# A hybrid convolution and gating layer: seven block products for eight, short filters for the convolution, and the out-projection in two passes

## The chip, the cores and the metric

The kernel runs on one core of a Trainium2 chip. A core has a matrix engine (TensorE, PE in the profile, with PEld for its weight loads), a vector engine (VectorE, DVE), a scalar engine (ScalarE, ACT), GpSimd (POOL) and SyncE (SP), which here only issues DMA transfers. Each engine runs its own list of instructions in order and waits on semaphores for the others. The metric is the device time of one execution in microseconds (us), lower is better; a comparison of two versions of this kernel counts as a difference from 0.2% on.

## The reference

One layer over 2048 tokens of width 1024, in fp32:

```
h = rms_norm(x, norm_g) * (1 + scale) + shift          # scale, shift, gate = silu(c) @ w_ada + b_ada
a, a_glu, a_gate, u, v, b_gate = split(h @ w_in)       # six column blocks of 1024 each
a   = a * sigmoid(a_glu)
a   = depthwise_conv(a, conv_w, 31 taps, centred) + conv_b
y_a = silu(layer_norm(a, ln_g, ln_b)) * silu(a_gate)
v   = layer_norm(v, sg_ln_g, sg_ln_b)                  # over the 1024 channels
v   = w_s[head] @ v + b_s                              # in chunks of 128 tokens, 8 heads of 128 channels
y_b = u * v * silu(b_gate)
x   = x + gate * (concat(y_a, y_b) @ w_out)            # w_out: 2048 x 1024
out = rms_norm(x, final_g)
```

## The kernel before

Every fp32 operand of a large product is split in two float32r parts, `hi` (an ACT copy) and `lo` (the rest, a DVE subtraction); a product is three matmuls, hi*hi, hi*lo and lo*hi, accumulated in one PSUM bank. One matmul takes 128 channels of weights and up to 512 tokens (or 128 tokens and 512 output columns).

The tokens are worked in two halves of 1024. `hhi` and `hlo` hold h of one half, channels on partitions. For every half:

- `v_group` (L254, matmuls at L243 to L245): v with tokens on partitions, in two column halves of eight banks each, 192 matmuls each.
- `conv_in(hf, j)` (L277) for each of 8 channel chunks j: `load_split` brings the weights of a_glu and a (two 512 KB loads, ACT copy at L120, DVE subtraction at L121), `proj` (L232 to L234) makes the columns. The first half takes 1040 tokens in blocks of 352, 352 and 336, since the filter reaches 15 tokens beyond, the second half 1008 in two blocks of 504.
- `conv(hf, j, g)` (L300): one ACT instruction for the first tap and 30 DVE instructions over 1024 tokens (L304) for the others.
- `gmlp(hf, j)`: b_gate (`pb`) and u (`pu`) in two blocks of 512, eight small fp32 matmuls `px` (L363) with w_s.
- `tail_of_half`: `conv_gate` (a_gate, `pag`), `conv_norm`, then the out-projection in groups of 2, 3 and 3 token tiles (L386 to L388). Each group loads and splits all of w_out again (16 chunks of 512 KB), the last group of the second half excepted.

All results between the stages stay on chip (`CY`, `VY`, `SQ`). The order on each engine is made when the program is built, by a list scheduler with costs of its own and priorities from the code; the start of the first half is ordered by hand on DVE.

Of the kernel before, what the change touches and what calls it, by code (L numbers as in the profile page):

```python
# [11 lines left out]
ALU = mybir.AluOpType  # L12

P = 128
D = 1024
KC = D // P
S = 2048
T = 1024
NTT = T // P
HALO = 16  # L20
TH = T + HALO
# [4 lines left out]
OFF = 1000  # L26
G0S, G0N, G1S = 0, 1, 4
# [3 lines left out]
def hybrid_layer_kernel(  # L31
# [20 lines left out]
    nc = tc.nc  # L52

    const = ctx.enter_context(tc.tile_pool(name="const", bufs=1))
    wst = ctx.enter_context(tc.tile_pool(name="wst", bufs=3))
    wsp = ctx.enter_context(tc.tile_pool(name="wsp", bufs=2))
    gpool = ctx.enter_context(tc.tile_pool(name="gpool", bufs=3))
    epool = ctx.enter_context(tc.tile_pool(name="epool", bufs=3))
    tabs = ctx.enter_context(tc.tile_pool(name="tabs", bufs=1))
    work = ctx.enter_context(tc.tile_pool(name="work", bufs=2))  # L60
    small = ctx.enter_context(tc.tile_pool(name="small", bufs=4))
    psum = ctx.enter_context(tc.tile_pool(name="psum", bufs=6, space=bass.MemoryType.PSUM))
    psumx = ctx.enter_context(tc.tile_pool(name="psumx", bufs=2, space=bass.MemoryType.PSUM))
# [7 lines left out]
    def wk(name, dt=F32):  # L71
        return work.tile([P, NG], dt, tag="wk", name=name)

    def ek(name, dt=F32):
        return epool.tile([P, 1056], dt, tag="e", name=name)

    def gk(name):
        return gpool.tile([P, 1056], F32, tag="g", name=name)

    tab = {}  # L80

    def load_wsT(hf):
        t = tabs.tile([P, KC, P], F32, tag="tab", name=f"wsT_{hf}")
        nc.sync.dma_start(t, w_sT)
        tab["wsT"] = t

    def load_fg(hf):
        t = tabs.tile([P, D], F32, tag="tab", name=f"fg_{hf}")
        nc.sync.dma_start(t, final_g.partition_broadcast(P))
        tab["fg"] = t  # L90
# [9 lines left out]
    btab = const.tile([P, KC, P], F32, name="btab")  # L100
    gate_b = const.tile([P, D], F32, name="gate_b")
# [5 lines left out]
    sv = const.tile([P, KC, 2 * PAD + 1], F32, name="sv")  # L107
    vst = const.tile([P, 4, NTT], F32, name="vst")

    hhi = const.tile([P, KC, TH], F32R, name="hhi")  # L110
    hlo = const.tile([P, KC, TH], F32R, name="hlo")
    CY = const.tile([P, KC, T], F32, name="CY")
    VY = const.tile([P, KC, T], F32, name="VY")
    SQ = const.tile([P, T], F32, name="SQ")

    normg, convb, clg, clb, slg, slb = (cols_sb[:, i, :] for i in range(6))

    def split(hi, lo, src, offset=OFF):
        with tc.high_priority(offset=offset):
            nc.scalar.activation(hi, src, AF.Copy)  # L120
            return nc.vector.tensor_tensor(out=lo, in0=src, in1=hi.bitcast(F32), op=ALU.subtract).ins  # L121

    def load(src, name):
        st = wst.tile([P, 1024], F32, tag="wst", name=f"st_{name}")
        nc.sync.dma_start(st, src)
        return st

    def split_w(st, a, name, offset=OFF):
        hi = wsp.tile([P, 1024], F32R, tag="whi", name=f"hi_{name}")
        lo = wsp.tile([P, 1024], F32R, tag="wlo", name=f"lo_{name}")  # L130
        split(hi, lo, st, offset)
        return hi.rearrange("p (a b) -> p a b", a=a), lo.rearrange("p (a b) -> p a b", a=a)

    def load_split(src, a, name):
        return split_w(load(src, name), a, name)

    nothing = lambda sqrt: None

    def rstd_of(var, n, name, np=P, fill=nothing):
        tile = lambda what: sm(f"{what}_{name}", n)[:np]  # L140
        sd, r0, t0, t1, r1 = (tile(what) for what in ("sd", "r0", "t0", "t1", "r1"))
        sqrt = nc.scalar.activation(sd, var, AF.Sqrt).ins
        fill(sqrt)
        nc.vector.reciprocal(out=r0, in_=sd)
        nc.vector.tensor_tensor(out=t0, in0=r0, in1=r0, op=ALU.mult)
        nc.vector.scalar_tensor_tensor(out=t1, in0=t0, scalar=-0.5, in1=var, op0=ALU.mult, op1=ALU.mult)
        nc.vector.scalar_tensor_tensor(out=r1, in0=t1, scalar=1.5, in1=r0, op0=ALU.add, op1=ALU.mult)
        return r1

    def spread(r, n, dst, name):  # L150
        """dst: the columns of r, one per 128 tokens, as rows on every partition."""
        ns = n // P
        dg = wk(f"dg_{name}")
        nc.vector.tensor_tensor(
            out=dg.rearrange("p (s t) -> p s t", t=P)[:, :ns, :],
            in0=ident[:, None, :].broadcast_to([P, ns, P]),
            in1=r[:, :, None].broadcast_to([P, ns, P]),
            op=ALU.mult,
        )
# [3 lines left out]
        return pr[:, :n]  # L163

    def rstd_rows(ssum, n, dst, name):
        """dst: 1/sqrt(mean + eps) of the columns of ssum summed over partitions, on every partition."""
        ns = n // P
        with tc.high_priority(offset=OFF):
            pc = xbank(f"pc_{name}")
            for s in range(ns):  # L170
                nc.tensor.matmul(pc[:, s : s + 1], ssum[:, s * P : s * P + P], ones[:, 0:1], start=True, stop=True)
            var = sm(f"var_{name}", ns)
            nc.vector.tensor_scalar(out=var, in0=pc[:, :ns], scalar1=1.0 / D, scalar2=EPS, op0=ALU.mult, op1=ALU.add)
            spread(rstd_of(var, ns, name), n, dst, name)

# [1 line left out]
    def mod_load(k):  # L177
        for i in range(2):
            nc.sync.dma_start(VY[:, (2 * k + i) % KC, :], wa_ss[i * KC + k])

    pms = {}

    def mod_half(k, i):
        if i == 0:
            pms[k] = sm(f"pm_{k}", 2)
        w = VY[:, (2 * k + i) % KC, :]
        nc.vector.scalar_tensor_tensor(
            out=w, in0=w, scalar=1.0, in1=c_row, op0=ALU.mult, op1=ALU.mult, accum_out=pms[k][:, i : i + 1]
        )
        if i == 1:  # L190
            nc.vector.tensor_tensor(out=mod[:, k, :], in0=pms[k], in1=bss_sb[:, k, :], op=ALU.add)
            nc.vector.scalar_tensor_tensor(
                out=gsc[:, k : k + 1],
                in0=mod[:, k, 1:2],
                scalar=1.0,
                in1=normg[:, k : k + 1],
                op0=ALU.add,
                op1=ALU.mult,
            )
# [526 lines left out]
    for hf in range(2):  # L726
# [15 lines left out]
        if hf == 0:  # L742
            x1_rstd()
# [69 lines left out]
```

## Time and profile before

| | |
|---|---|
| median of 3 runs | 1520.37 us (1520.12 to 1520.76) |
| profiled execution, first to last instruction | 1518.9 us |
| PE busy | 1490.1 us, 98% |
| DVE busy | 1189.2 us, 78% |
| ACT busy | 532.9 us, 35% |
| DMA | 142.91 MB, mean 94 GB/s |

The runs are given with what lies around the span of the profiled execution, 1.5 us. Busy times of PE contain the overlap of neighbouring matmuls, so the price of a matmul is read from the distance between the starts of a row of them, not from its duration.

### The profile page before, as it was taken

Reading aid. Unit: us, or ns where it says so; the run is one execution under the profiler, and the core shown is the slowest. Engines: PE = TensorE matmul, PEld = TensorE weight load, DVE = VectorE, ACT = ScalarE, POOL = GpSimd, SP = SyncE. Lnnn points to the kernel's source line nnn. Section 1 sums busy time; section 2 is a strip of 40 time slices with the busy share of each in tenths; the row PEclk is TensorE's granted clock in tenths of the full one; section 3 lists DMA queues with packets and bytes.
Section 4 is the critical chain, followed back from the end, with each engine's and each line's share of the span. In section 5 each row is a group of like instructions: output and inputs, shape, how many; then the busy total and the mean of one; then the engine's idle time right before and its main releaser. Section 6 shows DMA issues by size and latency. Waiting matters only on the chain.

```text
span 1518.9 us, 17158 instructions
## 1 busy us (share of the span) xinstructions
PE 1490.1 (98%) x6872; PEld 1236.4 (81%) x6872; DVE 1189.2 (78%) x1406; ACT 532.9 (35%) x799; POOL 16.6 (1%) x47
## 2 busy tenths in 40 slices
PE   5999999999999999999999999999999999999997
PEld 3798888999888877878888888888888878788876
DVE  7969999999999837887899703999999995477464
ACT  4331552222222336565423327212212133455331
POOL 0000000000000000000000000000000000000000
PEclk9999999999999999999999999999999999999999
DMA  9341121111112510654523311111111132147341
GB/s 362 128 152 43 42 70 56 57 55 57 56 56 78 172 43 28 221 181 139 166 86 109 125 42 54 45 42 43 55 42 42 46 107 84 42 125 226 104 141 42
DMA packets 42083, 142.91 MB, mean 94 GB/s; under 512 B 4449, under 2 KB 6657, under 8 KB 42002
## 3 DMA queue, kind: packets, MB, share of 16 engines
q1 hardware_dynamic: 39138, 131.74, 26.9%
q0 software_dynamic: 2864, 10.07, 1.8%
q8 instruction: 54, 0.88, 0.2%
q14 instruction: 27, 0.22, 0.0%
HBM read 133.40 MB, written 8.39 MB: 93 GB/s over the span
## 4 chain that ended last, share of the span: by engine, by line
PE 94%; DVE 3%; DMA 1%; ACT 1%; issue 1%; DVEq 0%; SPq 0%; ACTq 0%
PE po L386 7%; PE po L388 7%; PE po L387 7%; PE pag L234 4%; PE pb L234 4%; PE pu L234 4%; PE pg L233 4%; PE pa L233 4%; PE pu L233 4%; PE pg L232 4%; PE pa L232 4%; PE pb L233 4%; PE pa L234 4%; PE pg L234 4%; PE pag L233 4%; PE pag L232 4%
## 5 line engine op out<-in xcount | busy, mean ns | idle before, releaser
L304 DVE SCALAR_TENSOR_TENSOR CY<-g,cw_sb,CY 128x1024 f32<-128x1024 f32 x480 | 599.5, 1280 | 3.1 <-ACT CY L302 0.2
L387 PE MATMUL po<-lo_o,y_o 128*128 128x512 f32 x416 | 161.3, 394 | 0.5 <-DVE lo_o L121 0.5
L388 PE MATMUL po<-hi_o,y_o 128*128 128x512 f32 x416 | 161.1, 394 | 0.4 <-DVE y_o L121 0.4
L121 DVE TENSOR_TENSOR lo_o<-st_o,hi_o 128x1024 fp32r<-128x1024 f32 x80 | 97.8, 1223 | 51.8 <-ACT hi_o L120 50.9
L120 ACT ACTIVATE hi_o<-st_o 128x1024 fp32r<-128x1024 f32 x80 | 84.9, 1061 | 150.7 <-PE po L388 91.8
L386 PE MATMUL po<-hi_o,y_o 128*128 128x512 f32 x416 | 117.1, 395 | 1.3 <-ACT hi_o L120 1.2
L232 PE MATMUL pg<-hhi,hi_glu 128*128 128x352 f32 (+2 forms) x320 | 112.7, 352 | 0.0
L233 PE MATMUL pg<-hlo,hi_glu 128*128 128x352 f32 (+2 forms) x320 | 111.6, 349 | 0.0
L233 PE MATMUL pa<-hlo,hi_a 128*128 128x352 f32 (+2 forms) x320 | 111.5, 349 | 0.0
L232 PE MATMUL pa<-hhi,hi_a 128*128 128x352 f32 (+2 forms) x320 | 111.5, 348 | 0.0
L234 PE MATMUL pa<-hhi,lo_a 128*128 128x352 f32 (+2 forms) x320 | 111.4, 348 | 0.0
L234 PE MATMUL pg<-hhi,lo_glu 128*128 128x352 f32 (+2 forms) x320 | 111.0, 348 | 0.0
L243 PE MATMUL pv<-hi_v,hhi 128*128 128x512 f32 x256 | 101.1, 407 | 5.9 <-ACT hhi L211 5.9
L232 PE MATMUL pag<-hhi,hi_ag 128*128 128x512 f32 x256 | 103.4, 404 | 0.0
L234 PE MATMUL pag<-hhi,lo_ag 128*128 128x512 f32 x256 | 101.8, 399 | 0.0
L234 PE MATMUL pb<-hhi,lo_b 128*128 128x512 f32 x256 | 101.3, 396 | 0.0
L232 PE MATMUL pb<-hhi,hi_b 128*128 128x512 f32 x256 | 101.2, 395 | 0.0
L234 PE MATMUL pu<-hhi,lo_u 128*128 128x512 f32 x256 | 101.2, 396 | 0.0
L233 PE MATMUL pu<-hlo,hi_u 128*128 128x512 f32 x256 | 101.2, 395 | 0.0
L233 PE MATMUL pb<-hlo,hi_b 128*128 128x512 f32 x256 | 101.1, 395 | 0.0
L233 PE MATMUL pag<-hlo,hi_ag 128*128 128x512 f32 x256 | 101.1, 395 | 0.0
L244 PE MATMUL pv<-lo_v,hhi 128*128 128x512 f32 x256 | 101.0, 399 | 0.0
(208 smaller groups left out, 2686.6 us busy)
## 6 DMA issues: line engine op xcount, KB each, us to landing
st_o<-in_w_out_dram SPq DMA_DIRECT2D x88, 512.0 KB, 3.7
VY<-in_wa_ss_dram SPq DMA_DIRECT2D x16, 512.0 KB, 9.3
st_v<-in_w_v_dram SPq DMA_DIRECT2D x16, 512.0 KB, 3.7
st_glu<-in_w_main_dram SPq DMA_DIRECT2D x16, 512.0 KB, 3.6
st_a<-in_w_main_dram SPq DMA_DIRECT2D x16, 512.0 KB, 3.6
st_b<-in_w_main_dram SPq DMA_DIRECT2D x16, 512.0 KB, 3.6
st_u<-in_w_main_dram SPq DMA_DIRECT2D x16, 512.0 KB, 3.6
st_ag<-in_w_main_dram SPq DMA_DIRECT2D x16, 512.0 KB, 3.6
```

The source lines that it names most:

```text
L120: nc.scalar.activation(hi, src, AF.Copy)
L121: return nc.vector.tensor_tensor(out=lo, in0=src, in1=hi.bitcast(F32), op=ALU.subtract).ins
L232: nc.tensor.matmul(ps[:, :n], a, r0, start=(k == 0), stop=False)
L233: nc.tensor.matmul(ps[:, :n], a, r1, start=False, stop=False)
L234: nc.tensor.matmul(ps[:, :n], b, r0, start=False, stop=(k == KC - 1))
L243: nc.tensor.matmul(ps[t], a0, hi[:, kk, :], start=(k == 0), stop=False)
L244: nc.tensor.matmul(ps[t], a0, lo[:, kk, :], start=False, stop=False)
L304: nc.vector.scalar_tensor_tensor(out=acc, in0=g[:, i : i + T], scalar=cw_sb[:, j, i : i + 1], in1=acc, op0=ALU.mult, op1=ALU.add)
L386: nc.tensor.matmul(ps, yh, hi, start=st, stop=False)
L387: nc.tensor.matmul(ps, yh, lo, start=False, stop=False)
L388: nc.tensor.matmul(ps, yl, hi, start=False, stop=sp)
```

## The change

It rewrites the kernel's body. With the names of the new code:

- **Blocks.** The 1024 x 1024 product of a channel pair (two weight chunks of 128 columns, 1024 tokens) is cut in halves of the tokens, of the input channels and of the pair, and computed with seven block products for eight (`unit`, `product`, L432 to L472). The sums and differences of h (`S1` to `S4`) are built once for a half by `h_parts` and kept as split pairs in `H`; those of the weights are built by `weights` with four DVE subtractions for each pair. A unit uses three banks `p`, `t`, `q`; ACT copies one bank into another (`act(q, p, AF.Copy)`), and the last product M4 and the end of a unit are put behind the first product of the next one. A unit is 7 x 4 x 3 = 84 matmuls of 512; there are 8 units of `conv_in`, 8 of `gmlp` and 4 of `conv_gate` in each half. No tokens beyond the half are computed.
- **Weights.** In the first half (hf 0) each split weight operand (512 KB) is written to DRAM (`keep`, L138), and the second half reads it from there (L409, into a ring of 8 slots) and splits nothing.
- **v.** By blocks of 512 tokens, both column halves at once (`V.step`), 2 x 192 matmuls for a half as before, with plain split weights.
- **Convolution.** The gated input goes to DRAM and comes back with its 15 neighbours; the 31 taps are applied to alternating runs of 16 tokens: 46 DVE instructions over 496 or 528 tokens (L508, shapes 128x31x16 and 128x33x16) and one subtraction (L520) for each chunk, 16 chunks. It has the lowest priority of all work. The result goes to DRAM (`dC`).
- **Out-projection.** After both halves: a first pass over the gating part for four of five groups of token tiles, whose partial sums go to DRAM (`part_out`) and come back into PSUM (`part_in`), a pass for group 0 with both parts, and a second pass with the convolution's part. `w_out` is split once (`w_prepare`, in the second half's gmlp units) and kept.

```diff
...
-    def proj(ps, hi, lo, c0, n):
-        for k in range(KC):
-            a, b = hi[:, k, :], lo[:, k, :]
-            r0, r1 = hhi[:, k, c0 : c0 + n], hlo[:, k, c0 : c0 + n]
-            nc.tensor.matmul(ps[:, :n], a, r0, start=(k == 0), stop=False)
-            nc.tensor.matmul(ps[:, :n], a, r1, start=False, stop=False)
-            nc.tensor.matmul(ps[:, :n], b, r0, start=False, stop=(k == KC - 1))
...
+        before = dict(
+            M5=lambda: TT(out=b11, in0=b12, in1=b11, op=ALU.subtract),
+            M6=lambda: TT(out=b11, in0=b22, in1=b11, op=ALU.subtract),
+            M7=lambda: TT(out=b12, in0=b22, in1=b12, op=ALU.subtract),
+            M4=lambda: TT(out=b21, in0=b21, in1=b11, op=ALU.subtract),
+        )
+        src = dict(M1=b11, M5=b11, M6=b11, M2=b21, M3=b22, M7=b12, M4=b21)
+        for m in ORDER:
+            if m in before:
+                before[m]()
+            s = slot(f"w_{name}_{m}")
+            split(s, src[m])
+            keep((key, m), s)
+            yield s
...
+        product(p, "M1", next(ws), True)
+        act(q, p, AF.Copy)
+        flush()
+        product(t, "M5", next(ws), True)
+        act(m5, t, AF.Copy)
+        product(q, "M6", next(ws), False)
+        act(u2, q, AF.Copy)
+        product(p, "M2", next(ws), False)
+        y = start()
+        product(t, "M3", next(ws), False)
+        TT(out=y[:, :NG], in0=t, in1=u2, op=ALU.add)
+        product(q, "M7", next(ws), False)
+        TT(out=y[:, NG:], in0=q, in1=m5, op=ALU.add)
+        last = next(ws)
+
+        def rest():
+            product(q, "M4", last, False)
+            finish(p, q, y)
+
+        pending.append(rest)
...
-        for i in range(1, W):
-            nc.vector.scalar_tensor_tensor(
-                out=acc, in0=g[:, i : i + T], scalar=cw_sb[:, j, i : i + 1], in1=acc, op0=ALU.mult, op1=ALU.add
-            )
...
+            act(pairs(acc, 0), pairs(g[:, :n], 1), AF.Identity, bias=convb[:, j : j + 1], scale=cws[:, j, 0:1])
+            taps(0, 1, cws, 1, HT)
+            ne = n + HT - 2
+            TT(out=g[:, :ne], in0=g[:, :ne], in1=g[:, HT : HT + ne], op=ALU.subtract)
+            nc.scalar.copy(pairs(acc, 1), pairs(acc, 0))
+            taps(0, 0, cw_sb[:, :, :HT], 0, HT)
+            taps(1, 1, cw_sb[:, :, HT:], 0, W - HT)
+            nc.gpsimd.dma_start(dC[hf][j], acc)
...
```

What this moves is best seen in the engines' lists. On PE, in the first half's conv_in before the change, `pg` is a bank of a_glu, `hhi` and `hlo` the two parts of h:

```order
L232 MATMUL pg_3_0_1601<-hhi,hi_glu_3_1591 128x352
L233 MATMUL pg_3_0_1601<-hlo,hi_glu_3_1591 128x352
L234 MATMUL pg_3_0_1601<-hhi,lo_glu_3_1592 128x352
L232 MATMUL pg_3_0_1601<-hhi,hi_glu_3_1591 128x352
L233 MATMUL pg_3_0_1601<-hlo,hi_glu_3_1591 128x352
```

The same engine in the first half's unit a5 after the change: `pp`, `pt`, `pq` are the three banks, `H_S2` and `H_A22` blocks of h, `w_0_a5_M6` a slot of weights. M4 of the unit before (`pq_0_a4`) stands inside this unit's M6:

```order
L436 MATMUL pt_0_a5_2031<-H_S1_3_975,w_0_a5_M5_2074 128x512 x3
L436 MATMUL pq_0_a5_2032<-H_S2_0_797,w_0_a5_M6_2093 128x512 x3
L436 MATMUL pq_0_a5_2032<-H_S2_1_880,w_0_a5_M6_2093 128x512 x3
L436 MATMUL pq_0_a5_2032<-H_S2_2_963,w_0_a5_M6_2093 128x512 x3
L436 MATMUL pq_0_a5_2032<-H_S2_3_982,w_0_a5_M6_2093 128x512
L436 MATMUL pq_0_a4_1836<-H_A22_0_713,w_0_a4_M4_1971 128x512 x3
L436 MATMUL pq_0_a4_1836<-H_A22_1_785,w_0_a4_M4_1971 128x512 x3
```

Matmuls of 352 columns with eight channel chunks have become blocks of 512 columns with four. On DVE before, in the first half, where conv_in and gmlp alternate, taps (L304) of two chunks fill the list between a weight split (L121), a product with a bank (L295) and so on:

```order
L121 TENSOR_TENSOR lo_b_5_3117<-st_b_5_3114,hi_b_5_3116 128x1024
L304 SCALAR_TENSOR_TENSOR CY<-g_5_2265,cw_sb,CY 128x1024
L304 SCALAR_TENSOR_TENSOR CY<-g_6_2604,cw_sb,CY 128x1024
L295 TENSOR_TENSOR g_7_2943<-pa_7_0_3035,g_7_2943 128x352
L304 SCALAR_TENSOR_TENSOR CY<-g_5_2265,cw_sb,CY 128x1024
L304 SCALAR_TENSOR_TENSOR CY<-g_6_2604,cw_sb,CY 128x1024
```

After, in the first half between the ends of units a3 and a4 (`raw_0_a5` is the raw weight pair of unit a5, `w_0_a5_M5` its split operand, `acc_0_0` the convolution of chunk 0):

```order
L418 TENSOR_TENSOR raw_0_a5_2035<-raw_0_a5_2035 128x512
L508 SCALAR_TENSOR_TENSOR acc_0_0_1391<-gc_0_0_1388,cw_sb_99,acc_0_0_1391 128x31x16 x2
L420 TENSOR_TENSOR raw_0_a5_2035<-raw_0_a5_2035 128x512
L508 SCALAR_TENSOR_TENSOR acc_0_0_1391<-gc_0_0_1388,cw_sb_99,acc_0_0_1391 128x31x16
L134 TENSOR_TENSOR w_0_a5_M5_2074<-raw_0_a5_2035,w_0_a5_M5_2074 128x512
L508 SCALAR_TENSOR_TENSOR acc_0_0_1391<-gc_0_0_1388,cw_sb_99,acc_0_0_1391 128x31x16 x2
L419 TENSOR_TENSOR raw_0_a5_2035<-raw_0_a5_2035 128x512
L508 SCALAR_TENSOR_TENSOR acc_0_0_1391<-gc_0_0_1388,cw_sb_99,acc_0_0_1391 128x31x16 x3
```

A pair's weights now take eleven half-width DVE instructions (L418 to L421 and seven at L134), and the taps stand between them. On SP after the change, in the second half's gmlp units (before, this place had one 512 KB weight load, L125, after another), the weight reads (L409), the store of a split w_out chunk (L658), a result's store (L571) and a load of w_out (L654) share one queue:

```order
L658 DMA dW_o_1_7078<-ws_1_7075 128x2048
L409 DMA w_1_u3_M2_7341<-dW_('u', 3)_M2_3304 128x1024
L571 DMA dY_1_1_140<-us_1_1_7033 128x1024
L409 DMA w_1_u3_M3_7356<-dW_('u', 3)_M3_3322 128x1024
L409 DMA w_1_u3_M7_7371<-dW_('u', 3)_M7_3341 128x1024
L654 DMA wo_10_7227<-in_w_out_dram 128x1024
```

A weight read that stands behind a store waits until that store's data are made.

## Rows read from the trace of the kernel before

**Rows 1.** The page: span, busy time (share) and instructions of engines, and the chain's shares
```profile
span 1518.9 us, 17158 instructions
...
PE 1490.1 (98%) x6872; PEld 1236.4 (81%) x6872; DVE 1189.2 (78%) x1406; ACT 532.9 (35%) x799; POOL 16.6 (1%) x47
...
PE 94%; DVE 3%; DMA 1%; ACT 1%; issue 1%; DVEq 0%; SPq 0%; ACTq 0%
```
**Rows 2.** Waits of PE, longest first: engine, line, releaser: us, times, longest
```profile
PE pc_x L549 <- DVE SQ L546: 6.7, 1, 6.7
PE pv L243 <- ACT hhi L211: 5.9, 4, 2.9
```
**Rows 3.** PE in order of time: start, duration, engine, line, op, tiles, count
```profile
21.23 2.07 PE L243 MATMUL pv<-hi_v,hhi 128*128 128x512 f32 x4 [2.33 <-ACT hhi L211]
...
78.72 0.32 PE L232 MATMUL pg<-hhi,hi_glu 128*128 128x352 f32 x1
...
90.12 0.32 PE L232 MATMUL pa<-hhi,hi_a 128*128 128x352 f32 x1
...
217.56 1.95 PE L363 MATMUL px<-wsT,VY 128*128 128x128 f32 x16
219.26 0.41 PE L232 MATMUL pg<-hhi,hi_glu 128*128 128x352 f32 x1
...
335.94 0.39 PE L232 MATMUL pb<-hhi,hi_b 128*128 128x512 f32 x1
...
347.07 0.40 PE L232 MATMUL pu<-hhi,hi_u 128*128 128x512 f32 x1
...
1060.21 0.39 PE L232 MATMUL pa<-hhi,hi_a 128*128 128x504 f32 x1
...
1070.49 0.39 PE L232 MATMUL pb<-hhi,hi_b 128*128 128x512 f32 x1
...
1510.35 0.40 PE L388 MATMUL po<-hhi,yt 128*128 128x512 f32 x1
```
**Rows 4.** DVE by line and shape: count, busy us, mean ns, idle before it
```profile
L304 DVE SCALAR_TENSOR_TENSOR CY<-g,cw_sb,CY 128x1024 f32<-128x1024 f32 x480 | 599.5, 1280 | 3.1 <-ACT CY L302 0.2
L121 DVE TENSOR_TENSOR lo_o<-st_o,hi_o 128x1024 fp32r<-128x1024 f32 x80 | 97.8, 1223 | 51.8 <-ACT hi_o L120 50.9
L357 DVE TENSOR_TENSOR us<-pu,us 128x512 f32<-128x512 f32 x32 | 22.1, 690 | 17.4 <-PE pu L234 17.4
...
L187 DVE SCALAR_TENSOR_TENSOR VY<-VY,c_row 128x1024 f32<-128x1024 f32 x16 | 19.0, 1220 | 0.0
...
L208 DVE SCALAR_TENSOR_TENSOR CY<-CY,gsc,SQ 128x512 f32<-128x512 f32 x5 | 3.6, 749 | 1.9 <-ACT SQ L162 1.9
L208 DVE SCALAR_TENSOR_TENSOR CY<-CY,gsc,SQ 128x256 f32<-128x256 f32 x8 | 3.5, 479 | 0.0
...
L630 DVE TENSOR_TENSOR xh<-xh,mod 128x128 f32<-128x128 f32 x1 | 0.3, 291 | 0.0
...
L632 DVE TENSOR_TENSOR hlo<-xh,hhi 128x128 fp32r<-128x128 f32 x1 | 0.3, 283 | 0.0
```
**Rows 5.** Stretches: length, busy us of engines (instructions), PE clock, DMA share, GB/s
```profile
22.00:26.00 4.00, 4.00 (x12) 2.94 (x10) 3.90 (x10) 1.38 (x4) 0.00 (x0) 1.00 1.03 410
34.00:38.00 4.00, 2.89 (x6) 1.84 (x6) 3.52 (x9) 0.72 (x1) 0.00 (x0) 0.50 1.03 409
120.00:540.00 420.00, 420.00 (x2159) 368.66 (x2158) 381.82 (x378) 124.23 (x172) 0.56 (x5) 1.00 0.21 66
640.00:690.00 50.00, 49.38 (x213) 39.65 (x212) 44.31 (x84) 29.51 (x54) 1.22 (x3) 1.00 0.56 183
```
**Rows 6.** DMA issues of 512 KB: count, size, median us from issue to landing
```profile
st_o<-in_w_out_dram SPq DMA_DIRECT2D x88, 512.0 KB, 3.7
...
out_dram<-xo POOLq DMA_DIRECT2D x15, 512.0 KB, 3.1
```

More of the change, by code (lines that the diff above doesn't have):

```diff
@@ L12 @@
 ALU = mybir.AluOpType
+PSUM = bass.MemoryType.PSUM
+DRAM = bass.MemoryType.DRAM
 P = 128
@@ L123, in load @@
[L123 to L135, printed above, removed]
@@ L141, in rstd_of @@
[L141 to L143 removed]
+        sd, r0, t0, t1, r1 = (sm(f"{w}_{name}", n)[:np] for w in ("sd", "r0", "t0", "t1", "r1"))
+        act(sd, var, AF.Sqrt)
+        fill()
         nc.vector.reciprocal(out=r0, in_=sd)
[L145 to L146 removed]
@@ L162, in spread, with wa_tile @@
         nc.scalar.copy(dst, pr[:, :n])
[L163 to L179, printed above, removed]
-    pms = {}
+    pms = {}
+    wa_homes = [f"H_{b}_{k}" for k in range(KH) for b in ("S4", "A22")] * 2
+    wv_homes = [f"H_{b}_{k}" for k in (2, 1) for b in ("S1", "S2", "S3")] + ["H_S1_3", "H_S1_0"]
+    raw_homes = ["H_S2_0", "H_S3_0"]
+    was = {}
+    def wa_tile(k, i):
+        if (k, i) not in was:
+            w = hpool.tile([P, D], F32, tag=wa_homes.pop(0), name=f"wa_{k}_{i}")
+            nc.sync.dma_start(w, wa_ss[i * KC + k])
+            was[k, i] = w
+        return was[k, i]
     def mod_half(k, i):
@@ new lines, in product, with flush @@
+    def product(ps, m, s, first):
+        for k in range(KH):
+            h = H[BLK[m], k]
+            w0, w1 = (s[:, q, k * P : (k + 1) * P] for q in range(2))
+            mm = lambda w, a, st, sp: nc.tensor.matmul(ps, w, a, start=st, stop=sp, skip_group_check=True)
+            mm(w0, h[:, 0, :], first and k == 0, False)
+            mm(w0, h[:, 1, :], False, False)
+            mm(w1, h[:, 0, :], False, k == KH - 1)
+    pending = []
+    def flush():
+        while pending:
+            pending.pop(0)()
@@ L718, in hybrid_layer_kernel @@
[L718 to L738 removed]
+    nc.gpsimd.dma_start(cw_sb, conv_w)
@@ new lines, in hybrid_layer_kernel, with step, banks, by_rows @@
+    gate_b = sqp.tile([P, D], F32, tag="sq", name="gate_b")
+    dP = {}
+    steps, todo = [], set(range(len(GROUPS)))
+    def step():
+        while steps:
+            try:
+                next(steps[0])
+                return
+            except StopIteration:
+                steps.pop(0)
+    def banks(t):
+        return [bank(f"po_{t}_{d}") for d in range(2)]
+    def by_rows(gi, ps, e0, ys, st, sp):
+        for j in range(KC):
+            y, w = ys[j], w_o(e0 + j)
+            for t in range(GROUPS[gi][1]):
+                for d in range(2):
+                    out_mm(ps[t][d], y, w, t, d, st and j == 0, sp and j == KC - 1)
+            if j % 2 == 0:
+                step()
@@ new lines, in by_tile, with part_out @@
+    def by_tile(ps, ys, e0, t, st, sp, last=False):
+        order = [(d, j) for d in range(2) for j in range(KC)]
+        for d, j in order if last else sorted(order, key=lambda o: o[1]):
+            out_mm(ps[d], ys[j], w_o(e0 + j), t, d, st and j == 0, sp and j == KC - 1)
+    def part_out(t, ps):
+        st = ek(f"pb_{t}")
+        for d in range(2):
+            act(st[:, d * NG : (d + 1) * NG], ps[d], AF.Copy)
+        dP[t] = dt_(f"dP_{t}", [P, D])
+        nc.scalar.dma_start(dP[t], st)
```

1127 lines of the change are left out of this document (621 added, 506 removed).

## The prediction

> **What bounds the kernel now.** The page's first part comes first: over a span of 1518.9 us PE is busy 98% and DVE 78%, and the chain that ended last goes through PE for 94% [rows 1]. PE's waits, longest first, have 6.7 us at the top, and the next entry is four waits at the start [rows 2]: nothing stalls PE in the middle, so its matmuls must become fewer or shorter. Their price is read from PE in order of time, as the distance between starts [rows 3]. A block of 512 columns: (347.07 - 335.94)/48 = 0.232 us. The first half's conv_in, 48 of 352 and 24 of 336: (90.12 - 78.72)/72 = 0.158 us. The second half's, 45 of 504 between the two rows shown: (1070.49 - 1060.21)/45 = 0.228 us. The eight `px` products take (219.26 - 217.56) = 1.7 us, 16 records. The granted clock in the steady stretch is 1.00, the 2.4 GHz level [rows 5].
>
> The reader should then look at DVE, which is the second engine and gets new work: 381.8 us of the 420 us of the first half's middle [rows 5]. There is little left of its cover.
>
> **PE's gain.** Before, the projections a, a_glu, a_gate, u and b_gate are 768 + 1536 = 2304 matmuls of 512 (534.3 us), 768 of 504 (175.4) and 1152 of 352 or 336 (182.4), together 892.1 us. After, 40 units of 84: 3360 x 0.2319 = 779.2 us. That is 112.9 us less. v (768) and the out-projection (1536) keep their numbers; sixteen more px products (3.4 us at 1.7 for eight) stand against the removed small matmuls of the bias tables and are taken as equal. 1518.9 - 112.9 = **1406.0 us**, if everything else stays hidden.
>
> **What DVE gains and loses.** Two sizes of the same operation as a tap, 256 and 512 columns, take 479 and 749 ns, and the tap of 1024 takes 1280 [rows 4]: a line of 0.214 us + 1.04 ns for each column through the last two. By it a tap of 496 costs 0.73 and of 528 0.77 us. The convolution before: 480 x 1.280 + 17 others = 617 us; after: 368 x 0.73 + 368 x 0.77 + 16 x 1.24 = 572 us. The taps read and write runs of 16. The one row with such runs, L632 (eight runs of 16), takes 283 ns where the neighbour of equal size takes 291 [rows 4]: no penalty seen, and up to some 4% of a tap is within that. A half-width subtraction costs 0.69 us (L357), one of full width 1.22 (L121) [rows 4]. A unit has eleven of them for weights in the first half (7.6 us; before, two splits of 1.22 for each chunk pair and product, 4.9), and three to four for ends of about 0.69 to 0.75 us.
>
> Counted by stretch in the order of DVE's new list, with these prices: from the end of unit a0 to that of s6, 19 units of the first half, DVE has 229 taps (167.4 us), 199 weight operations (137.3), 69 of unit ends (47.6), gating (25.4), H (12) and about 8.5 of others, **398.2 us**. PE has there 19 x 84 x 0.2319 = 370.1 plus px and v's blocks that fall in it, 386.6. So DVE becomes the bound of the first half: **+11.6 us**. The taps have the lowest priority, but the list is fixed when the program is built: a tap that stands ahead of a weight split is done before it, and PE waits behind both. From s6 to the second half's first unit (v again) it is 107.1 against 108.8, a tie. In the second half no weights are split: 350.2 against 385.3, so 35 us of slack. In the out stage DVE has 329.5 against PE's 381; its first 115 to 131 us, the rest of the taps, the norm and its splits, must end within pass 1 (146 us), again close. For those two near ties **+5 us** (0 if the list is well ordered, 10 if each is missed by 3%).
>
> **The copies between banks.** Each unit copies p into q on ACT, and M6 accumulates onto that copy; M4 of the previous unit and its end stand in between. A product lasts 12 x 0.232 = 2.8 us, and M5 (2.8 us) stands between the copy and its use, with ACT at 35% [rows 1]. Hidden, 0; if that cover is lost, one or two us for each unit (a rival).
>
> **The start.** Before, PE's first v matmul is at 21.23 and v's first group ends at 78.72 [rows 3]: 192 matmuls take 44.5, so 34.2 us are not v. After, v's first block does both column halves with twice the DVE work at each of four steps (four L187 of 1.22 to 1.30, four half-width splits, H's parts): 11.7 us a step against PE's 11.1 (48 x 0.232); from a first matmul near 23 it would end near 70. The row statistic of the second block of tokens goes through DRAM and back: two transfers of at least 3.1 and 3.7 us [rows 6], so PE gets on near 76 and ends v at about 121.5. Less 384 x 0.2319 = 89, some 32.5 are not v. I take 0, bounds -5 and +10. In 34 to 38 us, behind the idle time of the start, the granted clock is 0.50, the 1.2 GHz level [rows 5]; a longer gap would be paid for in that coin too.
>
> **Transfers.** The split weights, written once and read once, and the round trips of the convolution and of the partial sums bring the bytes from 142.9 to about 380 MB (counted from the new program's transfers). The rows give two rates: 410 GB/s at the start where the queues are full, and 183 at a busy share of 0.56, that is 327 GB/s if the share went to 1 [rows 5]. The tightest place is the second half's gmlp and gate units from u1 on: 78.3 MB on SP's queue (weight reads, w_out's loads and stores of its split parts) and 4.2 of the convolution, 82.5 MB while PE has 227.7 us. That needs 362 GB/s. At 410 it takes 201 us and is hidden; at 327 it takes 252 and costs 25. SP's queue is in order, so a weight read behind a store of a w_out chunk waits for that chunk's DVE splits too. I take **+10 us**, nearer the good end, because the ring of eight slots reads one unit ahead. The Trainium skill, page "DMA: Bandwidth & Descriptors", section "Where 436 GB/s comes from", puts one core's share of memory at about 358 GB/s; by it the place would take an estimated 230 us and cost some 3. The trace shows 410 for this core alone [rows 5], so by the row that share is no wall here; only loads were seen at that rate, and these transfers hold stores too.
>
> **The out stage and the tail.** Each w_out part must come every 4.2 us (1 MB, 250 GB/s), and partial sums return into PSUM before the pass that adds to them: a load of 512 KB takes 3.7 us [rows 6], one wait for each group not quite covered: **+4 us** (0 to 12). PE's last matmul starts 8.5 us before the end [rows 1, 3], and what follows it is unchanged.
>
> **Sum.** 1406.0 + 11.6 (DVE, first half) + 5 (ties) + 10 (transfers) + 4 (out) + 0 (start) = 1436.6 us of span; with the 1.5 us by which the runs' median exceeds the span, **1438 us**, 5.4% less. A measurement of this kernel can tell about 0.2% from no change, 3 us.
>
> **Rivals.**
> *All is hidden.* DVE's list has its slack where PE needs it and the queues run at 410 GB/s: 1406 + 1.5, near 1408, up to 1425. For it: PE's waits before are nearly nothing at a DVE share of 91% [rows 2, 5]. Against: 398.2 us of DVE's work do not fit in 386.6.
>
> *Transfers bind.* At 327 GB/s in the second half (+25 instead of 10) and with out's loads late (+12 instead of 4), plus reads that stand behind stores: 1460 to 1500. For it: 380 MB over a span of 1.4 ms is a mean of 265 GB/s, three times what was ever asked of the queues for long. Against: 410 was reached.
>
> *Slower: short runs are dear.* If a tap over 31 or 33 runs of 16 costs a fraction x more than the line says, DVE's surplus grows by 167 x in the first half, by about 149 x in v's and the out stage, and in the second half by 254 x less its 35 us of slack; 316 x + 254 x - 35 reaches the 82 us that separate the sum from before at x = 0.205, a tap of 0.92 us for 0.765. At 25% it gives 1545, at 40% about 1630. For it: only one row, with eight runs, speaks of runs. Against: that row, which shows nothing at all.
>
> *The unit's chain stalls PE.* Copy, M6, the end in DVE's order behind taps, and the bank given back: 1 to 2 us at each of 40 units is 40 to 80, 1480 to 1520; above 2 us each it is no gain. For it: three banks a unit and in-order DVE. Against: M5 and the next unit's M1 lie between.
>
> **How the numbers follow.** My forecast, 1425 to 1460, 0.50; all hidden 0.15; transfers bind 0.17; short runs dear 0.10, of which 0.08 slower; the unit's chain 0.08, of which 0.04 slower, 0.02 about the same and 0.02 faster. Faster thus 0.50 + 0.15 + 0.17 + 0.02 + 0.02 = 0.86, within 0.2% 0.02, slower 0.12. The range 1400 to 1500 holds the first three; what is left out, 0.18, lies above. The range of the likeliest alone is 1425 to 1460.
>
> **What the profile after would show.** PE: about 5,700 to 5,800 matmuls of 512, 0.232 us from start to start, clock at 1.00. DVE near 1296 us busy, 90% of the span, and without idle time in the first half's units; PE's longest waits there, on splits (L134) or unit ends (L465, L479). Taps (L508) of 0.73 and 0.77 us. In the second half's gmlp units PE waits, if for anything, on SP's reads (L409), at a DMA share above 0.8. Wrong if taps exceed 0.80 us, if PE waits in every unit for ACT's copies, or if waits lie at the start or in the out stage for more than 10 us.

## The result and the profile after

The changed kernel takes 1392.68 us (median of 4 runs, 1391.67 to 1393.18); beside it the kernel before took 1520.53 us. The ratio is 0.9158, 95% interval 0.9145 to 0.9171: 8.4% faster where 5.4% was forecast, and faster than the rival in which everything is hidden (1408). The time lies below the stated range.

The page of the profiled execution, first and fourth part, against [rows 1]:

```profile
span 1390.7 us, 17690 instructions
...
PE 1348.8 (97%) x6026; PEld 1111.9 (80%) x6026; DVE 1162.2 (84%) x1984; ACT 572.5 (41%) x1098; POOL 33.6 (2%) x82
...
PE 59%; issue 28%; DVE 7%; DMA 4%; ACT 1%; POOL 0%; SPq 0%; DVEq 0%; ACTq 0%; POOLq 0%
```

PE is still the bound. DVE is busy 1162 us, not the 1296 that were counted for it. The chain's 28% of "issue" is PE's own time too: in those stretches the chain runs along PE's list with nothing waited for.

PE's waits, longest first (us in total, times, longest), against [rows 2]:

```profile
PE po L671 <- DMA wr<-dW_o: 10.5, 1, 10.5
PE pv L365 <- ACT H_A L271: 8.4, 2, 5.3
PE pc_x L217 <- DVE rows L215: 7.0, 1, 7.0
PE pr_x L163 <- DVE dg_x L156: 3.4, 1, 3.4
PE pcr L727 <- DMA c_row<-in_c_dram: 2.4, 1, 2.4
PE pq_s L436 <- DVE sag L465: 0.8, 1, 0.8
PE po L671 <- ACT sag L532: 0.7, 1, 0.7
PE pmean L604 <- DVE t_o L148: 0.4, 1, 0.4
```

The second to the fifth lie in the first 75 us, the first and the seventh at the start of the out stage, and from 121 to 984 us there is none: PE waits nowhere for a split (L134) or a weight read (L409). Stretches of the changed kernel, first half's units, second v, second half's units, out stage (columns as in [rows 5]; after the length the busy us of PE, PEld, DVE, ACT, POOL):

```profile
124.00:517.00 393.00, 393.00 (x1801) 326.87 (x1801) 360.43 (x588) 190.54 (x351) 5.62 (x14) 1.00 0.86 310
517.00:607.00 90.00, 90.00 (x399) 74.53 (x398) 82.13 (x134) 37.83 (x83) 2.23 (x6) 1.00 0.68 245
607.00:1003.00 396.00, 395.22 (x1811) 328.62 (x1810) 331.35 (x493) 122.80 (x220) 11.67 (x28) 1.00 0.87 314
1003.00:1382.00 379.00, 367.43 (x1606) 300.40 (x1606) 295.70 (x584) 156.41 (x310) 10.71 (x21) 0.98 0.58 204
```

DVE has 33 us to spare in the first row, where the sum had it 11.6 us over. PE in order of time, inside a unit:

```profile
193.40 2.88 PE L436 MATMUL pq_a<-H_S,w_a_M 128*128 128x512 f32 x12
196.12 2.88 PE L436 MATMUL pp_a<-H_A,w_a_M 128*128 128x512 f32 x12
198.84 2.88 PE L436 MATMUL pq_a<-H_A,w_a_M 128*128 128x512 f32 x12
```

A product of 12 matmuls starts every 2.72 us: (196.12 - 193.40)/12 = 0.2267 us for a matmul of 512 columns. Before it was 0.2319 [rows 3]. The matmul itself got cheaper by 2.2%, in v and in the out-projection as well as in the units, and nothing in the prediction had a place for that: the means over the two whole traces are 0.2319 and 0.2268, and 5664 x 0.0051 = 28.9 us. DVE by line and shape, and a run of taps on DVE in order of time, against [rows 4]:

```profile
L508 DVE SCALAR_TENSOR_TENSOR acc<-gc,cw_sb,acc 128x528 f32<-128x528 f32 x248 | 174.8, 760 | 0.4
L508 DVE SCALAR_TENSOR_TENSOR acc<-gc,cw_sb,acc 128x496 f32<-128x496 f32 x248 | 171.1, 728 | 3.5 <-ACT acc L521 3.2
```

```profile
708.77 9.59 DVE L508 SCALAR_TENSOR_TENSOR acc<-gc,cw_sb,acc 128x528 f32<-128x528 f32 x14
718.28 0.68 DVE L463 TENSOR_TENSOR g<-pt_a,u_a 128x512 f32<-128x512 f32 x1
```

The forecast durations of a tap (0.77 and 0.73 us) are met to 0.01, so the short runs cost nothing that shows. But 14 taps in a row take 718.28 - 708.77 = 9.51 us, 0.679 us each: one begins 80 ns before the duration of the one ahead of it is over. The kernel before had the same, (348.53 - 338.96)/8 = 1.196 us for each of eight taps with a duration of 1.280:

```profile
338.96 9.65 DVE L304 SCALAR_TENSOR_TENSOR CY<-g,cw_sb,CY 128x1024 f32<-128x1024 f32 x8
348.53 1.22 DVE L121 TENSOR_TENSOR lo_glu<-st_glu,hi_glu 128x1024 fp32r<-128x1024 f32 x1
```

### The profile page after: what moved, and what is told of

It reads as the page before. It is cut to its first block, busy times and chain, and to the rows that moved or that the text cites. A ratio compares the mean times of both kernels' runs of the same rounds, so it can differ in the third digit from the quotient of the medians.

```text
span 1390.7 us, 17690 instructions
## 1 busy us (share of the span) xinstructions
PE 1348.8 (97%) x6026; PEld 1111.9 (80%) x6026; DVE 1162.2 (84%) x1984; ACT 572.5 (41%) x1098; POOL 33.6 (2%) x82
## 4 chain that ended last, share of the span: by engine, by line
PE 59%; issue 28%; DVE 7%; DMA 4%; ACT 1%; POOL 0%; SPq 0%; DVEq 0%; ACTq 0%; POOLq 0%
PE pq_a L436 9%; PE pq_u L436 6%; PE pp_a L436 6%; PE pt_a L436 6%; PE pp_u L436 5%; PE pt_u L436 4%; PE pv L365 3%; PE pv L366 3%; PE pv L367 3%; PE pq_s L436 2%; DVE acc L508 2%; PE pt_s L436 2%; PE pp_s L436 2%; PE po L673 1%; PE po L672 1%
## 5 line engine op out<-in xcount | busy, mean ns | idle before, releaser
L508 DVE SCALAR_TENSOR_TENSOR acc<-gc,cw_sb,acc 128x496 f32<-128x496 f32 (+1 forms) x496 | 345.9, 744 | 3.9 <-ACT acc L521 3.2
L671 PE MATMUL po<-wr,y 128*128 128x512 f32 x512 | 201.5, 395 | 11.1 <-DMA wr<-dW_o 10.5
L508 DVE SCALAR_TENSOR_TENSOR acc<-gc,cws,acc 128x496 f32<-128x496 f32 (+1 forms) x240 | 179.6, 748 | 33.5 <-ACT acc L517 29.4
L672 PE MATMUL po<-wr,y 128*128 128x512 f32 x512 | 201.5, 394 | 0.0
L673 PE MATMUL po<-wr,y 128*128 128x512 f32 x512 | 201.4, 394 | 0.0
L671 PEld LDWEIGHTS po<-wr,y 128*128 128x128 f32 x512 | 96.8, 189 | 33.0 <-DMA wr<-dW_o 10.9
L672 PEld LDWEIGHTS po<-wr,y 128*128 128x128 f32 x512 | 96.8, 189 | 21.4 <-issue 1.0
L673 PEld LDWEIGHTS po<-wr,y 128*128 128x128 f32 x512 | 96.7, 189 | 21.0 <-issue 0.7
L436 PE MATMUL pt_u<-H_S,w_u_M 128*128 128x512 f32 x384 | 94.0, 392 | 0.0
L436 PE MATMUL pq_u<-H_S,w_u_M 128*128 128x512 f32 x384 | 93.8, 391 | 0.0
L436 PE MATMUL pp_u<-H_A,w_u_M 128*128 128x512 f32 x384 | 92.9, 390 | 0.0
L436 PE MATMUL pp_a<-H_A,w_a_M 128*128 128x512 f32 x384 | 92.7, 389 | 0.0
L436 PE MATMUL pq_a<-H_S,w_a_M 128*128 128x512 f32 x384 | 92.5, 389 | 0.0
L436 PE MATMUL pt_a<-H_S,w_a_M 128*128 128x512 f32 x384 | 92.5, 390 | 0.0
L548 ACT ACTIVATE vc<-vc,vstat 128x128 f32<-128x128 f32 x128 | 51.0, 481 | 15.1 <-DMA vc<-dV 14.2
```

The costliest lines, as they stand in the source:

```text
L436: mm = lambda w, a, st, sp: nc.tensor.matmul(ps, w, a, start=st, stop=sp, skip_group_check=True)
L508: STT(out=pairs(acc, h), in0=pairs(g[:, i : i + n], at), scalar=tab[:, j, i : i + 1], in1=pairs(acc, h), op0=ALU.mult, op1=ALU.add,)
L548: act(vch[:, t, :], vch[:, t, :], AF.Identity, bias=vstat[:, 8 + t : 9 + t], scale=vstat[:, t : t + 1])
L671: nc.tensor.matmul(ps, yh, hi, start=st, stop=False, skip_group_check=True)
L672: nc.tensor.matmul(ps, yh, lo, start=False, stop=False, skip_group_check=True)
L673: nc.tensor.matmul(ps, yl, hi, start=False, stop=sp, skip_group_check=True)
```

## The experiments

**Where the operands lie.** The price of a matmul of 512 columns changed in every stage, so its cause is common to all. The start-to-start times of all matmuls in both traces, in the order of the programs, showed a pattern: before, the times within one product run from 226 to 240 ns and repeat from product to product, most of them to 1 or 2 ns, whatever DVE, ACT and the queues do; after, nearly all are 226 or 227. The addresses in the programs as built differ in one respect. After the change all moving and stationary operands begin at the same place modulo 256 bytes. Before, hhi began 32 bytes off the weights', and its rows of 1040 tokens shift the place by 64 bytes with every chunk; in the out-projection, 420 of 1536 agree, and there the mean was 228 ns against 233. Two kernels test it, from both sides. The first is a_shift32:

```diff
-    small = pool("small", 4)
+    small = pool("small", 4); padp = pool("padp", 1); pad = padp.tile([P, 8], F32, name="pad")
```

> The changed kernel with 32 bytes of padding for each partition put between the small tiles and the pool that holds H; nothing else. In the changed kernel the moving and the stationary operand of every large matmul begin at addresses that are equal modulo 256 bytes, and a matmul of 512 columns takes 0.227 us from start to start; before the change they were equal for few (420 of 1536 in the out-projection, where the trace shows 0.228 us), and the others took 0.232 to 0.233. Theory A (the relative address of the two operands sets the price): 4320 of the 5664 matmuls (all 3360 of the units, 576 of v, 384 of the out-projection) go from 0.227 to about 0.232, 4320 x 0.0055 = 24 us more, 1416 us; the other 1344 stay at 0.227 in the same trace. Rival B (the matmul got cheaper for another reason: one width, blocks of four chunks, less work of DVE's in long instructions): no change, 1393 us, and one price for all.

Measured: 1419.92 us (1419.41 to 1420.89), 27.2 us above the changed kernel. PE in order of time in a unit of this run:

```profile
200.27 2.96 PE L436 MATMUL pp_a<-H_A,w_a_M 128*128 128x512 f32 x12
203.07 2.96 PE L436 MATMUL pq_a<-H_A,w_a_M 128*128 128x512 f32 x12
205.87 2.96 PE L436 MATMUL pt_a<-H_S,w_a_M 128*128 128x512 f32 x12
```

2.80 us a product, 0.2333 a matmul; 4320 x (0.2333 - 0.2267) = 28.5 us, the whole of what was measured. The 192 matmuls of v and 1152 of the out-projection whose operands moved together, or not at all, stayed at 0.227 to 0.228 in the same trace where they stand among their like. Behind a border, where the matmuls ahead have operands that lie otherwise, it is different: in the out-projection the two chunks that disagree take 0.233, and the first five to seven matmuls of an equal chunk behind such a border still take 0.231 to 0.232. So already here the neighbours count. 32 bytes of padding cost 2%; rival B falls.

The other side is b_align, the kernel before with other addresses:

```diff
...
-    epool = ctx.enter_context(tc.tile_pool(name="epool", bufs=3))
+    padp = ctx.enter_context(tc.tile_pool(name="padp", bufs=1)); pad2 = padp.tile([P, 32], F32, name="pad2"); epool = ctx.enter_context(tc.tile_pool(name="epool", bufs=3))
...
-        return epool.tile([P, 1056], dt, tag="e", name=name)
+        return epool.tile([P, 1088], dt, tag="e", name=name)
...
-    hhi = const.tile([P, KC, TH], F32R, name="hhi")
-    hlo = const.tile([P, KC, TH], F32R, name="hlo")
+    hhi = const.tile([P, KC, TH + 16], F32R, name="hhi")
+    hlo = const.tile([P, KC, TH + 16], F32R, name="hlo"); pad = const.tile([P, 56], F32, name="pad")
...
```

> The kernel before with padding alone: rows of hhi and hlo 1056 tokens wide for 1040, a pad behind them and one ahead of the pool of the y tiles, so that both operands' addresses are equal modulo 256 bytes for 2508 matmuls of 512 columns more (1152 of the projections, 384 of v, 972 of the out-projection). Theory A (relative address): these go from 0.2325 to about 0.2275, 2508 x 0.005 = 12.5 us less, about 1508 us, and even and odd channel chunks show two prices in one product. Rival B (another reason): 1520 us, one price.

Measured: 1513.3 us (1512.33 to 1514.37), ratio to before 0.995 (0.9935 to 0.9965). The sign was right, the size not, and the detail was wrong: in the out-projection the matmuls that now agree take 227 to 228 ns as expected, but in the projections the chunks that agree took 233 ns and those that don't, 231. There the phase still changed by 128 bytes from chunk to chunk. The first matmuls of `pb` and, 48 later, of `pu` show a block that is no cheaper than before, (345.82 - 334.69)/48 = 0.2319 us:

```profile
334.69 0.39 PE L232 MATMUL pb<-hhi,hi_b 128*128 128x512 f32 x1
...
345.82 0.39 PE L232 MATMUL pu<-hhi,hi_u 128*128 128x512 f32 x1
```

So agreement within one matmul is not enough. The next run, b_align2, makes the neighbours agree too (and halves the bias table to make room); the cut shows it against b_align:

```diff
-    btab = const.tile([P, KC, P], F32, name="btab")
+    btab = const.tile([P, KC // 2, P], F32, name="btab")
...
-    hhi = const.tile([P, KC, TH + 16], F32R, name="hhi")
+    hhi = const.tile([P, KC, TH + 48], F32R, name="hhi")
...
```

> The kernel before with padding as in the run b_align, but with rows of hhi and hlo 1088 tokens wide, so that all 4608 matmuls of 512 columns have both operands at the same address modulo 256 bytes and successive operands too (in b_align the even and the odd channel chunks differed by 128 bytes, and the projections' matmuls took 233 and 231 ns there, against 228 in the out-projection, where neighbours agree). To make room the bias table of the gate holds four of its eight heads, so four heads get another head's bias. Theory A2 (a matmul of 512 columns takes 0.227 us when the two operands, and those of its neighbours, agree modulo 256 bytes): 3072 matmuls of the projections and of v go from 0.2325 to 0.2272 and 1100 of the out-projection from 0.2325 to 0.2275, 16.3 + 5.5 = 22 us less than before, about 1499 us. Rival B2 (agreement does not matter in the projections, something else in their loop does): about 1512 us as in b_align, the projections' price at 0.231 to 0.233.

Measured: 1496.86 us (1496.03 to 1497.79), 0.9837 of before (0.982 to 0.9853), 24.9 us less, with nothing changed but addresses and the bias table. PE in order of time, the first matmul of `pb` and, 48 matmuls later, the first of `pu`, as in [rows 3]:

```profile
332.25 0.39 PE L232 MATMUL pb<-hhi,hi_b 128*128 128x512 f32 x1
...
343.16 0.39 PE L232 MATMUL pu<-hhi,hi_u 128*128 128x512 f32 x1
```

(343.16 - 332.25)/48 = 0.2273 us, with the old loops, the old blocks and all of the old work around them. Theory A2 holds: the price is set by where the operands lie, and the new kernel's blocks happened to lie well. That part of the gain is luck: neither the change as described nor the prediction has a word on addresses.

**Is DVE the bound of the first half?** In the run a_notaps the taps are left out:

```diff
-                for i in range(i0, n_taps):
+                for i in range(i0, i0):
```

> The changed kernel without the taps: of the convolution's 46 DVE instructions for each chunk none is left, only its first tap, its difference, its copies and its transfers; so the convolution's values are left out. 526 us of DVE's work go. Theory C (the taps fill gaps that PE never sees): 0 to 5 us less than the changed kernel (its longest wait in the out stage may shorten, since a DVE list without taps is free earlier there). The prediction's term (DVE sets the pace of the first half's units): the units would get shorter by 11 us or more; since PE has no wait of 0.3 us in them, I expect them to stay at 393 us for 19 units.

Measured: 1398.96 us (1395.65 to 1400.44), not faster. The first half's units of this run, columns as above:

```profile
123.00:518.00 395.00, 395.00 (x1810) 328.60 (x1809) 234.58 (x372) 198.60 (x365) 10.49 (x26) 1.00 0.88 321
```

From the units' first matmul to v's first of the second half it is 518.99 - 122.28 = 396.7 us here and 517.12 - 120.42 = 396.7 in the changed kernel: 127 us less work of DVE's in that stretch changes nothing. Behind it, the second half's units took 401 us for 396 (3.0 us of that are new waits for DVE, whose list has another order), the out stage 375.2 for 378.5, and the first unit began 1.9 us later; why the median is 6 us higher was not followed up further. The prediction's term is gone. The other direction, more work for DVE, is the run a_direct, which undoes the short filters:

```diff
-            taps(0, 1, cws, 1, HT)
...
-            taps(0, 0, cw_sb[:, :, :HT], 0, HT)
-            taps(1, 1, cw_sb[:, :, HT:], 0, W - HT)
+            act(acc, g[:, :n], AF.Identity, bias=convb[:, j : j + 1], scale=cw_sb[:, j, 0:1])
+            for i in range(1, W):
+                STT(out=acc, in0=g[:, i : i + n], scalar=cw_sb[:, j, i : i + 1], in1=acc, op0=ALU.mult, op1=ALU.add)
...
```

> The changed kernel with the convolution done by 30 full taps over 992 or 1056 tokens, as before the change, in place of the short filters; all else as it is, the result the same. By the starts of neighbouring taps in the traces (1.196 us for 1024 columns, 0.646 and 0.680 for 496 and 528) a chunk costs DVE 35.9 us for 31.7, 67 us more in all, about 35 of them in the first half's units. Theory C (an instruction of DVE costs its start-to-start distance, so DVE has 33 us to spare in the 400 us of the first half, 57 in the 360 of the second): 0 to 10 us more, PE's new waits in the first half's units. The sum as predicted (an instruction costs its duration, DVE was already the bound there): 35 us or more on top.

Measured: 1439.72 us (1437.87 to 1441.89), 47 us more: neither theory had it right. PE's waits, longest first:

```profile
PE pmean L600 <- DVE sq L597: 20.6, 1, 20.6
PE po L667 <- ACT y L133: 12.3, 2, 8.3
PE pc L612 <- DVE sq L608: 10.3, 1, 10.3
```

All lie in the out stage, from 1292 us on (lines are four lower in this kernel). In the units PE waits for DVE 1.2 us in all. The taps have the lowest priority, so the list lets the units pass and carries the taps on: 120 of 480 were still to do when the units ended, the last one began at 1281.70, and the norm that needs them held PE up. With the short filters 102 of 736 were left, and the last one began at 1124.42. From the first to the last matmul of `po` the out stage takes 422.7 us here and 378.5 in the changed kernel, 44 of the 47 us; PE waits 49.1 us in it for 11.6, and from 1275 us on the granted clock is 0.50, the 1.2 GHz level, for 47.8 us. So what counts for DVE is not the stretch in which the taps stand but its whole work up to the second pass: there the short filters are worth 47 us in this list, and taking away more than they do (a_notaps) gives nothing.

**Does PE set the pace of the units?** The run a_eight has an eighth product in each unit:

```diff
-        product(t, "M5", next(ws), True)
+        w5 = next(ws)
+        product(t, "M5", w5, True)
+        product(t, "M5", w5, True)
```

> The changed kernel with an eighth product in each unit: M5 is computed twice into the same bank, so the result stays. PE bound: 40 units x 12 matmuls x 0.2268 = 109 us more, less what DVE's taps, which are behind PE in the out stage, no longer hold back there (at most a few us): about 1495 to 1502 us. If another engine set the pace of the units, less than 90 us more.

Measured in one run: 1496.88 us, 104.2 us more, with 480 matmuls more (480 x 0.2267 = 108.8); the out stage's first wait is 6.9 us here for 10.5, which is most of the difference. Seven products for eight are worth what their matmuls cost.

**Transfers.** The run a_dma adds copies that nothing reads:

```diff
+                if m in ("M1", "M3"):
+                    nc.sync.dma_start(dt_(f"jk_{name}_{m}", [P, D]), dW[key, m])
```

> The changed kernel with two copies of 512 KB from DRAM to DRAM added to SP's queue in each unit of the second half, 20 MB in all; nothing reads them. In the second half the profile has 320 GB/s at a busy share of 0.88, and PE waits for no weight read. With 1 MB more for each unit of 19 us that becomes 375 GB/s moved. Theory F (the queues reach 410 GB/s in the middle of the kernel too): 0 to 3 us more than the changed kernel. Rival G (327 GB/s is the limit there, the lower bound of the prediction): the second half's gmlp and gate units take 92.5 MB / 327 = 283 us for the 229 they have, 50 us more.

Measured: 1395.69 us (1394.79 to 1397.6), 3.0 us more. The run does not answer its question: the copies had nothing to wait for but the store of the weights, and the list put them into the first half, from 119 us on. So 20 MB more are nearly free there (354 GB/s at a share of 0.95 from 121 to 516 us, for 310 at 0.86 without them), and nothing is said of the second half. The changed kernel's own trace says it, in the gmlp units of the second half:

```profile
759.00:935.00 176.00, 176.00 (x831) 147.23 (x830) 146.47 (x210) 60.81 (x107) 4.99 (x12) 1.00 0.96 360
```

360 GB/s at a share of 0.96, and PE busy 176.00 of 176: hidden, though with little left. Over the whole place that the prediction meant, 759 to 986 us, it is 361 GB/s in 227 us: 82 MB, as it had counted (82.5). The bound of 327 GB/s was wrong: it scaled one stretch of the old kernel, 183 GB/s at a share of 0.56, up to a share of 1, and the same scaling of the changed kernel's stretches above gives 352 to 375. What made the old stretch move less at its share is not shown.

**The wait at the start of the out stage.** SP and PE around it in the changed kernel, in order of time:

```profile
995.90 14.61 SPq L640 DMA_DIRECT2D yb<-dY  x6
...
1013.90 0.42 SPq L533 DMA_DIRECT2D dS<-sag  x1
1014.36 1.74 SPq L640 DMA_DIRECT2D y<-dY  x2
1016.20 4.22 SPq L665 DMA_DIRECT2D wr<-dW_o  x6
```

```profile
1026.04 0.80 PE L671 MATMUL po<-wr,y 128*128 128x512 f32 x1 [10.46 <-DMA wr<-dW_o]
1026.63 0.63 PE L672 MATMUL po<-wr,y 128*128 128x512 f32 x1
1027.06 0.63 PE L673 MATMUL po<-wr,y 128*128 128x512 f32 x1
```

The six loads of w_out (`wr`) stand on SP behind the stores of the last gate unit (`dS`) and behind y loads of this group (`y`) and of the next (`yb`). From 1017.8 us, within the idle 10.5 us, to 1031.5 the granted clock is 0.50, the 1.2 GHz level, and the matmuls start 0.43 us apart (1027.06 - 1026.63); 13 are slower by this, 2.6 us in all. The run a_early changes SP's order:

```diff
-            nc.sync.dma_start(dS[hf][j], a)
+            (nc.scalar if hf and i == KC // 2 - 1 else nc.sync).dma_start(dS[hf][j], a)
...
+    first.enter_context(tc.manual_schedule(engines={mybir.EngineType.SP}))
...
-        ys = [y_b(gi, j) for j in range(KC)]
+        ys = [(y_b(gi, j), n or w_o(KC + j))[0] for j in range(KC)]
...
```

> The changed kernel with the order of SP's queue at the start of the out stage changed: the loads of w_out's chunks 2 to 7 of the gating part stand between the y loads of the first group, ahead of the next group's y loads, and the last gate unit's two stores are issued by ACT. In the changed kernel PE waits 10.5 us there for the first of these loads (issued at 1016.2, landed at 1026.0), and its clock is 0.50 for some 10 us behind the wait, which makes about 14 matmuls 0.2 us longer. Theory D (the load stands behind loads and stores on SP that wait for buffers): the wait goes, 10.5 + 3 = 13 us less, about 1380 us. Rival E (the space that the load goes to is free only behind the last unit, or y's splits on ACT are late next): 0 to 5 us less.

Measured: 1394.34 us (1393.43 to 1400.26), no gain: the wait for w_out is gone, and PE waits 6.7 us for ACT's split of y and 3.7 for DVE's, 10.4 in all. ACT stands there for 11.2 us at the convolution's first instruction (L517), which waits for the store of the last chunk's result, and y's split (L133) is behind it:

```profile
1025.38 0.82 ACT L517 ACTIVATE acc<-gc,cols_sb,cws 128x528 f32<-128x528 f32 x1 [11.23 <-DMA dC<-acc]
1026.11 1.34 ACT L133 ACTIVATE y<-y 128x384 fp32r<-128x384 f32 x3
```

The next run, a_early3, has, against that:

```diff
...
-        ys = [(y_b(gi, j), n or w_o(KC + j))[0] for j in range(KC)]
+            with tc.manual_schedule(engines={mybir.EngineType.Activation}):
+                ys = [y_b(gi, j) for j in range(KC)]
+                conv(1, KC - 2)
+            conv(1, KC - 1)
+            for j in range(2, KC):
+                w_o(KC + j)
...
```

> The changed kernel, with the out stage's first loads reordered as in the run a_early (in which the load was no longer waited for, and y's splits were instead, for 10.4 us, since they stood on ACT behind the convolution's first instruction of chunk 6, which waited for the store of chunk 5's result), and with all of the first group's y loads ahead of the chunks of w_out and its splits ahead of that instruction on ACT. Theory D: both waits go, PE's clock stays at 1.00 there, 10 to 13 us less than the changed kernel, about 1381 us. Rival E (the chunks arrive too late anyway, since six loads of 1 MB share the queues with the convolution's transfers): 0 to 5 us less.

Measured: 1393.31 us (1392.2 to 1393.82), again no gain: waits of 2.95 us at 1044.9 and 2.54 at 1059.7 for the second group's y (5.7 us in three places), and one of 2.1 at 1318.4 for DVE, each of the three with 3.4 us at a granted clock of 0.50 beside it.

Last, in a_early4, the first y loads of the second group before the last three chunks:

```diff
-            for j in range(2, KC):
-                w_o(KC + j)
+            for j in range(2, 5):
+                w_o(KC + j)
+            early = [y_b(1, j) for j in range(KH)]
+            for j in range(5, KC):
+                w_o(KC + j)
...
```

> The run a_early3 once more (there the 10.5 us wait for w_out's chunk went and PE waited 6.5 us in three places 30 us later, for the second group's y splits, whose loads came behind the six chunks; the time stayed), with the first four y loads of the second group ahead of the last three chunks. Theory D: these waits go too, 5 to 10 us less than the changed kernel. Rival E (the loads of that stretch take the queues' whole rate whatever their order, so a wait comes back elsewhere): within 3 us of the changed kernel.

Measured: 1389.09 us (1388.41 to 1390.91), 3.6 us less than the changed kernel, 0.26%. PE's waits in the out stage:

```profile
PE po L671 <- DMA wr<-dW_o: 3.6, 1, 3.6
...
PE po L673 <- DVE y L134: 1.4, 1, 1.4
```

Both theories have a part: half of the wait went, a third of it stays, for the chunks that now come last. In the profiled executions the out stage, from the first to the last matmul of `po`, takes 378.5 us in the changed kernel, in a_early and in a_early3, and 371.8 here: 6.7 us less, of which 1.9 are lost at the start, where the first unit begins at 122.34 us for 120.42. It is the fastest version of this study, though the 0.26% is barely above what can be told: the intervals of the two ratios to the kernel before touch (0.9123 to 0.9151 here, 0.9145 to 0.9171 for the changed kernel).

## Why the prediction was wrong

By its own steps:

- **PE's gain, -112.9 us:** right as a count; a_eight shows that twelve matmuls a unit cost what PE's row says. The price taken for each of the 5664 matmuls that remain, 0.2319 us, is the step that failed: it was carried over from the kernel before as if it belonged to the operation. It measured 0.2267, 28.9 us less in all, and a_shift32, b_align and b_align2 show that the operands' addresses set it.
- **DVE as the bound of the first half, +11.6 us:** wrong. The counts were right (228 taps were done in the 393 us of the units for 229 counted) and so were the durations, 1290 us in sum after for 1296 forecast; but instructions of DVE overlap by some 80 ns, so the sum of durations isn't the time. The row of the old taps had it: 480 of 1280 ns are 614 us, and their busy time is 599.5 [rows 4]. In order of time eight of them take 1.196 us each, as shown above. The Trainium skill, page "VectorE: DVE Perf Modes", section "Two Vector instructions with no wait between them", gives a model by which an instruction is held until all earlier ones have finished only where operands start in other groups of 32 partitions than those of the instructions before it, or where the one in front of it mixes two such groups. The taps here, which all use all 128 partitions, agree with it at 0.679 us from start to start for 0.760 of duration. a_notaps shows that the term is nothing.
- **The near ties, +5:** nothing; PE doesn't wait for DVE in either stretch.
- **Transfers, +10:** nothing. The bytes were counted right; the lower of its two rates was wrong. By the share of memory that the prediction cites from the Trainium skill, page "DMA: Bandwidth & Descriptors", section "Where 436 GB/s comes from", the place would have cost an estimated 3 us; the trace has 361 GB/s over its 227 us, and no wait of PE's for a transfer.
- **The out stage, +4:** too small: waits of 10.5, 0.7 and 0.4 us and 2.6 us of half clock, 14.2. The mechanism wasn't foreseen: the loads' place in SP's list is behind the next group's loads, and a_early, which changes it, takes this wait away. More than 10 us of waits in the out stage was one of the prediction's own signs of being wrong.
- **The start, 0:** right. v ends at 120.42, 120.42 - 384 x 0.2267 = 33.4 us that aren't v, for 34.2 before; the second block's wait of 5.3 us is the one that was described, though its first transfer took 9.4 us and not 3.1 or so.
- **The copies between banks, 0,** and **short runs, 0:** right.

With what was measured in their place: 1406.0 - 28.9 + 14.2 - 0.8 = 1390.5 us, and the span is 1390.7; the terms themselves are not known to 0.2 us, so that they meet so well is partly luck. The time came out below the case in which all is hidden because of the first of these points alone; with most of the matmuls at the old price (a_shift32, 1420 us) it lies inside the range, in the case where all is hidden, which had 0.15, and not in the one that was forecast.

## What to carry to other kernels

Read the price of an operation from start to start, also on DVE, and never add up durations: overlap is in the difference of busy time and count times mean. Before a price is carried from one kernel to another, look whether it is constant within the old one; matmuls of one shape that take 226 to 240 ns in a fixed pattern have a cause in the program, and here it was worth 1.6% in the old kernel for padding, and for the room that the padding needs (half a bias table, so a usable version has to find it elsewhere). A wait at the border of two stages that is taken away in the order of the queues has to be looked for again 10 to 30 us later: of three orders here two gained nothing.

## What was not expected of the hardware

- A float32r matmul of 512 columns starts 226.7 ns after the one ahead when moving and stationary operands, its own and its neighbours', begin at the same place modulo 256 bytes of a partition; 32 bytes apart it took 233.3 (a_shift32), and 231 to 233 where only every other chunk agreed (b_align). Matmuls of 352 columns hardly changed (161 ns before, 160 in b_align2), but that is no clean test: their second block begins 1408 bytes into a row, which is not a multiple of 256. Which part of the memory causes it, and whether 256 bytes is the exact period, stays open: other distances were not tried one by one.
- One core moved 361 GB/s for 227 us with loads and stores mixed, at a busy share of 0.96 (changed kernel, 759 to 986 us).
